# Token tiles read in quarters behind the first weights, in a one-core diffusion block

## The chip, the core and the metric

The kernel runs on one core of a Trainium2 chip. The core has five engines, each with an instruction stream of its own that is worked off in the order in which it was compiled: TensorE (PE in the profile, its weight loads PEld), VectorE (DVE), ScalarE (ACT), GpSimd (POOL) and SyncE (SP). SP computes nothing here: it issues the transfers between the chip's main memory and the core's on-chip memory. The metric is the device time of one execution in microseconds (us).

## What is computed

The reference is one layer of a diffusion transformer block in float32, with 1024 tokens of width 1024 on a grid of 16 rows by 64 columns, and 256 context tokens:

```python
sh1, sc1, g1, sh2, sc2, g2 = split(silu(c) @ w_mod + b_mod, 6)     # adaLN; likewise for c_ctx
h  = rms_norm(x, norm1) * (1 + sc1) + sh1
hc = rms_norm(ctx, norm1) * (1 + csc1) + csh1
q, k, v = split(h @ w_qkv, 3); kc, vc = (hc @ w_k), (hc @ w_v)     # q, k, kc: RMS norm per head
y = neighbourhood_attention(q, k, v, kc, vc, rpb) @ w_o            # window 8 x 16, plus the context
x = x + g1 * y
x = x + g2 * conv_ffn(rms_norm(x, norm2) * (1 + sc2) + sh2, w_up, conv, w_down)
```

## The kernel before

A float32 product is made of three products of float32r operands: each operand is split into a high part (a copy by ACT) and a low part (original minus high part, by DVE or POOL), and PE adds up high x high, high x low and low x high.

The program is written with a tile framework. Its scheduler lays out the whole program once, at compile time: it keeps its own account of when operands will be there, and puts each engine's instructions into a fixed order, by the order of the source where several are ready. On the chip an engine doesn't leave that order: if the next instruction's operand is late, everything behind it on this engine waits. A tile pool hands out a fixed number of buffers for each tag, and the next tile of a tag waits until an older one is read out.

The change lies in the first hundred microseconds of the program, in these steps:

1. **Shift and scale (lines 197 to 270).** `load_m` (L203) reads w_mod in 16 pieces `mraw` of 512 KB. For each, ACT makes the high part (`mh`, L246), DVE the low part (`ml`, L247), and PE multiplies both by the conditioning vector (L257, L258). Every fourth piece a row goes through ACT (L262) and PE (L264). The result is `s1` (L268) and `b1` (L270); no token can be modulated before b1.
2. **The first weights.** `load_w` (L211) reads w_qkv of the first pair of heads in four loads of 384 KB into the same buffers as the pieces of w_mod. `prep_w` (L138) splits them: high parts on DVE (L144), low parts on POOL (L147).
3. **Tokens.** There are ten tiles of 128 tokens, two of the context and eight of x, in the order TORD = 8, 9, 0, ..., 7. `load_x` (L165) reads one (512 KB) into one of four buffers of tag `pt`. A tile of x holds, for each of the 16 grid rows, 8 neighbouring columns, so its source is 16 runs of 32 KB, 256 KB apart. `stats_x` (L173) squares and sums it on ACT (L155; the squares themselves go to a tile that is written later anyway), takes the power -1/2 on POOL (L157) and scales the tile on DVE (L176). `transpose_x` (L178) transposes it on PE (L182), modulates it (DVE L189, ACT L191), and splits it into `hth` (ACT L193) and `htl` (DVE or POOL, L194). These twenty results lie in 20 slots of 4 KB per partition, which later parts of the kernel use again; `order` (L118) says which.
4. **First projection.** `qkv_gen(0)` (L294) makes the product of each tile with the first weights: 24 matmuls on PE (L301, L303, L305) into one of two PSUM buffers `pq`, then norms and copies (ACT L322, L329; DVE L323, L324, L330, L334, L340; POOL L325). A product's `pq` comes free when the last of these has read it. In the loop at L549 the product of tile i - AHEAD stands behind the transposes of tile i; AHEAD is 1.
5. **Loads for the attention** (L273 to L278, L365, L134, L463): the masks `mi` and `mr`, the bias table `rpb` of the first head with its sums on POOL (L371, L375), the raw weights of the second pair, and the rest of w_mod, which DVE multiplies and adds up a little at a time (`macc`, L469 and L471). The memory of these tiles comes free only when the buffers of step 2 are read out (L275 waits for L147).

Seven small constants (L223 to L235, together under 80 KB) are issued by SP between the pieces 10 and 11 of w_mod. The attention of the first head begins with the transposes at L384; from there on projections, attention, output projection and the feed-forward part follow, which the change leaves as they are.

Of the kernel before, what the change touches and what calls it, by code (L numbers as in the profile page):

```python
# [10 lines left out]
F32 = mybir.dt.float32  # L11
F32R = mybir.dt.float32r
AF = mybir.ActivationFunctionType
# [5 lines left out]
P = 128  # L19
D = 1024  # L20
KC = D // P
SEQ = 1024
CTX = 256
ROWS, COLS = 16, 64
# [6 lines left out]
NF = DFF // P  # L31
EPS = 1e-6
SCALE = DH ** -0.5
NT = NB + CTX // P
TORD = [NB, NB + 1] + list(range(NB))
BIG = 1e30
HALF = 512
MW = 256
AHEAD = 1
WB = 21  # L40
FT = -1
WS = 512
# [9 lines left out]
WD, SQD = range(8), ()  # L52
# [9 lines left out]
def block_kernel(ctx, tc, x, ctxt, cc, w_mod, b_col, b_row, n1, n2, w_qkv, gains, rpb_t, mask_i, mask_r, w_o,  # L62
                 w_up, conv_w, conv_b, w_down, comb, out):
    nc = tc.nc
    PE, ACT, DVE, POOL, SP = nc.tensor, nc.scalar, nc.vector, nc.gpsimd, nc.sync
# [11 lines left out]
    def f(ap):  # L77
        return ap.bitcast(F32)

    xv = x.rearrange("(r b j) d -> b r j d", r=ROWS, b=NB, j=8)  # L80
    ov = out.rearrange("(r b j) d -> b r j d", r=ROWS, b=NB, j=8)

    const = ctx.enter_context(pool("const"))
# [31 lines left out]
    def slot(tag, name, dt=F32R, shape=(P, D)):  # L115
        return big.tile(list(shape), dt, tag=tag, bufs=SLOTS[tag], name=name)

    order = ["gb", "t4", "t4"] + ["wa"] * 6 + ["wx"] * 2 + ["r4"] + ["rh"] * 4 + ["rl"] * 4  # L118
    hth, htl = {}, {}
    for i, t in enumerate(TORD):  # L120
        hth[t] = slot(order[2 * i], f"hth{t}", shape=(P, KC, P))
        htl[t] = slot(order[2 * i + 1], f"htl{t}", shape=(P, KC, P))
# [6 lines left out]
    ps = pstack.enter_context(pool("ps", space=PSUM))  # L129
# [20 lines left out]
    def norm_rows(t, sq, ss, sqd=False):  # L150
        if sqd:
            DVE.tensor_tensor_reduce(out=sq, in0=t, in1=t, scale=1.0, scalar=0.0, op0=ALU.mult, op1=ALU.add,
                                     accum_out=ss)
        else:
            ACT.activation(sq, t, AF.Square, accum_out=ss)  # L155
        DVE.tensor_scalar(ss, ss, 1.0 / D, EPS, ALU.mult, ALU.add)
        POOL.tensor_tensor(ss, ss, mhalf[:, 0:1], ALU.pow)  # L157

    # adaLN of the attention branch, normalised and modulated tokens, transposed and split
    att = ExitStack()  # L160
    sa = att.enter_context(pool("sa"))

    xin = {}

    def load_x(t):  # L165
        xt = sa.tile([P, D], F32, tag="pt", bufs=4, name=f"xt{t}")
        if t < NB:
            SP.dma_start(out=xt, in_=xv[t])
        else:
            SP.dma_start(out=xt, in_=ctxt[(t - NB) * P:(t - NB + 1) * P, :])  # L170
        xin[t] = xt

    def stats_x(t):  # L173
        ss = const.tile([P, 1], F32, tag="ss", bufs=3, name=f"ss{t}")
        norm_rows(xin[t], htl[t].rearrange("p a b -> p (a b)"), ss, t in SQD)
        DVE.tensor_scalar(xin[t], xin[t], ss, None, ALU.mult)  # L176

    def transpose_x(t):  # L178
# [17 lines left out]

    with pool("sm") as sm:
        segs = [1024, 1536, 0, 512]
        MB, PTM = 8, (8, 9, 10)
        AH = MB + len(PTM)  # L200
        mraw = {}

        def load_m(i):  # L203
            si, k2 = divmod(i, 4)
            if i in PTM:
                mraw[i] = sa.tile([P, 2, HALF], F32, tag="pt", bufs=4, name=f"mraw{i}")
            else:
                mraw[i] = sm.tile([P, 2, HALF], F32, tag="mraw", bufs=MB, name=f"mraw{i}")
            SP.dma_start(out=mraw[i], in_=wm[:, 2 * k2:2 * k2 + 2, segs[si]:segs[si] + HALF])

        def load_w(i):  # L211
            raw = sm.tile([P, 2, 3 * P], F32, tag="mraw", bufs=MB, name=f"wr0_{i}")
            SP.dma_start(out=raw, in_=w_qkv[0, 2 * i:2 * i + 2].rearrange("k p n -> p k n"))
            for k in range(2):
                prep_w(0, 2 * i + k, raw[:, k, :])

        for i in range(MB):
            load_m(i)
        load_x(TORD[0])
        for i in range(MB, AH):  # L220
            load_m(i)
        comb_sb = const.tile([4, 2], F32, name="comb_sb")
        SP.dma_start(out=comb_sb, in_=comb)  # L223
        bcol = const.tile([P, 48], F32, name="bcol")
        SP.dma_start(out=bcol, in_=b_col)
        n1c = const.tile([P, KC], F32, name="n1c")
        SP.dma_start(out=n1c, in_=n1)
        n2c = const.tile([P, KC], F32, name="n2c")
        SP.dma_start(out=n2c, in_=n2)
        gain_sb = const.tile([P, 2], F32, name="gain_sb")  # L230
        SP.dma_start(out=gain_sb, in_=gains)
        cw = const.tile([P, NF, 3], F32, name="cw")
        SP.dma_start(out=cw, in_=conv_w)
        cb = const.tile([P, NF], F32, name="cb")
        SP.dma_start(out=cb, in_=conv_b)  # L235
        qg = const.tile([P, 1], F32, name="qg")
        DVE.tensor_scalar(qg, gain_sb[:, 0:1], -SCALE, None, ALU.mult)
        kg = gain_sb[:, 1:2]
        pc = ps.tile([P, 2, KC, 2], F32, tag="po", bufs=1, name="pc")
        for si in range(4):  # L240
            pm = ps.tile([4, HALF], F32, tag="pq", bufs=2, name=f"pm{si}")
            for k2 in range(4):
                i = 4 * si + k2
                mh = sm.tile([P, 2, HALF], F32R, tag="mh", bufs=2, name=f"mh{i}")
                ml = sm.tile([P, 2, HALF], F32R, tag="ml", bufs=2, name=f"ml{i}")
                ACT.activation(mh, mraw[i], AF.Copy)  # L246
                DVE.tensor_tensor(ml, mraw[i], f(mh), ALU.subtract)  # L247
                if i + AH < 16:
                    load_m(i + AH)
                if 16 <= i + AH < 20:  # L250
                    load_w(i + AH - 16)
                if i in PTM:
                    load_x(TORD[1 + i - PTM[0]])
                for k in range(2):
                    kk = 2 * k2 + k
                    lw = c4[:, kk, :, :].rearrange("p a b -> p (a b)")
                    PE.matmul(pm, lw, mh[:, k, :], start=(kk == 0), stop=False)  # L257
                    PE.matmul(pm, lw, ml[:, k, :], start=False, stop=(kk == KC - 1))  # L258
                if i in (13, 14):
                    stats_x(TORD[i - 13])  # L260
            row = sm.tile([4, HALF], F32, tag="mrow", bufs=1, name=f"mrow{si}")
            ACT.activation(row, pm, AF.Copy)  # L262
            for k in range(4):
                PE.matmul(pc[:, si // 2, 4 * (si % 2) + k, :], row[:, k * P:(k + 1) * P], comb_sb, start=True,  # L264
                          stop=True)
            if si == 1:
                DVE.tensor_tensor(s1, pc[:, 0], bcol[:, 8:16].unsqueeze(2).broadcast_to([P, KC, 2]), ALU.add)
                DVE.scalar_tensor_tensor(s1, s1, 1.0, n1c.unsqueeze(2).broadcast_to([P, KC, 2]), ALU.add, ALU.mult)  # L268
            if si == 3:
                DVE.tensor_tensor(b1, pc[:, 1], bcol[:, 0:8].unsqueeze(2).broadcast_to([P, KC, 2]), ALU.add)  # L270

    # attention, with the projections of the next pair of heads in between
    sb = att.enter_context(pool("att"))  # L273
    mi = sb.tile([P, 3 * P], F32, name="mi")
    SP.dma_start(out=mi, in_=mask_i)  # L275
# [179 lines left out]
        DVE.tensor_tensor(res[a:b], po[a:b], tmp[a:b], ALU.add)  # L455
        SP.dma_start(out=o_dram[p, a:b, u * 2 * P:(u + 1) * 2 * P], in_=res[a:b])

    # adaLN of the rest, a little at a time
    def mod_gen():
        order = [2, 3, 4, 5]  # L460
        for sgi in order:
# [27 lines left out]
                        DVE.scalar_tensor_tensor(dst, dst, 1.0, n2c[:, nk * hf:nk * (hf + 1)], ALU.add, ALU.mult)  # L489
                yield  # L490

    # output projection: its first half runs beside the attention of the last heads
    xpool = ctx.enter_context(ExitStack())
    x1, wo, g1b, xsb = {}, [], [], []
    HP = NPAIR // 2
# [50 lines left out]
    mg = mod_gen()  # L546
    fill = qkv_gen(0)
    stats_x(TORD[2])
    for i, t in enumerate(TORD):  # L549
        transpose_x(t)  # L550
        if i + 4 < NT:
            load_x(TORD[i + 4])
        if i + 3 < NT:
            stats_x(TORD[i + 3])
        if i >= AHEAD:
            while (0, 1, TORD[i - AHEAD]) not in vt:
                next(fill)
# [17 lines left out]
    for si in range(ns + 4):  # L575
        if si < ns:
            p, h, t = steps[si]
# [7 lines left out]
        if si + 1 < ns and steps[si + 1][2] % 2 == 0:  # L585
            p, h, t = steps[si + 1]
# [6 lines left out]
        if 0 <= si - 3 < ns and steps[si - 3][2] % 2 == 1:  # L593
            p, h, t = steps[si - 3]
# [7 lines left out]
    filler(10 ** 6)  # L602
    att.close()

    # rest of the output projection, second norm, operands of the Winograd form (seven products of halves
    # in place of eight) of the up projection: A is w_up^T in 2 x 2 blocks, B the tokens in 2 x 2 blocks
    ff = ctx.enter_context(ExitStack())
    usb = ff.enter_context(pool("ffn"))
    BT = {}
# [1 line left out]
    for i, op in enumerate(WORD):  # L611
        for j in range(4):
            tag = btags[4 * i + j]
# [3 lines left out]
            else:  # L617
                BT[op, hl, kk] = usb.tile([P, 2, HALF], F32R, tag=tag, bufs=12 if tag == "bA" else 10,
                                          name=f"b{op}{hl}{kk}")
# [193 lines left out]
    nprep, gens, g, y, late = 2, {}, {}, {}, []  # L813
# [166 lines left out]
```

## Time and profile before

| | |
|---|---|
| median of three runs | 1492.29 us (1489.33 to 1492.66) |
| span of the profiled execution, first to last instruction | 1491.8 us |
| PE busy | 1386.5 us (93%) |
| DVE busy | 1208.1 us (81%) |
| ACT busy | 738.1 us (49%) |
| POOL busy | 805.7 us (54%) |
| moved by the DMA engines | 153.27 MB, 103 GB/s on the mean |

The profile is of one execution. Its own time is its span; the median of the runs lies 0.5 us above that. Busy times are sums over the whole span, which has stages with different limits: a stage is read from its own stretch. "A <- B" in a list of waits says that A stood idle until B was done.

### The profile page before, as it was taken

How to read it: one execution, taken by the hardware profiler on the slowest of the kernel's cores; microseconds unless marked ns; L12 is line 12 of the kernel's file. 1: busy time of each engine (PE TensorE's matmuls, PEld its weight loads, DVE VectorE, ACT ScalarE, POOL GpSimd, SP SyncE). 2: the span in 40 equal slices, each digit the busy share in tenths (PEclk: the TensorE clock that was granted, in tenths of full speed). 3: DMA queues.
4: the chain of work that ended last, by engine and by line, in shares of the span. 5: the costliest groups of instructions: out<-in, count | busy, mean ns of one | idle time of the engine just before them, and what ended most of it. 6: DMA issues, size and time to landing. Idle time of an engine off the chain costs nothing.

```text
span 1491.8 us, 22077 instructions
## 1 busy us (share of the span) xinstructions
PE 1386.5 (93%) x7396; PEld 1200.0 (80%) x7396; DVE 1208.1 (81%) x2392; ACT 738.1 (49%) x1601; POOL 805.7 (54%) x672
## 2 busy tenths in 40 slices
PE   6689999999999999999996999999999987898998
PEld 2589889898989899888885777888888865686887
DVE  6778878888888878866589889788877779988884
ACT  6575645555565656645465434344343334244541
POOL 1455544545454546744368545555545568474872
PEclk9899999999999999999997999999999998899999
DMA  9612221313131202262132132233332347433343
GB/s 315 161 37 60 64 87 55 92 51 103 49 101 45 77 14 73 69 152 76 50 129 99 64 108 101 96 106 106 107 106 99 106 137 286 155 100 127 110 131 105
DMA packets 84827, 153.27 MB, mean 103 GB/s; under 512 B 9945, under 2 KB 49001, under 8 KB 84713
## 3 DMA queue, kind: packets, MB, share of 16 engines
q1 hardware_dynamic: 84712, 151.86, 32.7%
q8 instruction: 58, 0.95, 0.3%
q14 instruction: 57, 0.46, 0.1%
HBM read 119.05 MB, written 32.78 MB: 102 GB/s over the span
## 4 chain that ended last, share of the span: by engine, by line
PE 60%; DVE 20%; DMA 7%; POOL 5%; issue 4%; ACT 3%; SPq 0%; DVEq 0%; POOLq 0%; ACTq 0%
PE pg L740 8%; PE pa L740 7%; PE sw L740 6%; PE pq L301 5%; PE pq L303 5%; PE pq L305 5%; DMA mr<-in_w_mod_dram 2%; DVE y L787 2%; DVE p L410 2%; POOL u L688 2%; PE s L398 2%; PE po L448 2%; PE po L449 2%; PE py L525 2%; PE py L526 2%
## 5 line engine op out<-in xcount | busy, mean ns | idle before, releaser
L688 POOL TENSOR_TENSOR u<-ur,u 128x512 fp32r<-128x512 f32 x154 | 231.9, 1519 | 176.8 <-ACT u L687 175.1
L417 POOL TENSOR_TENSOR p<-p,m 128x640 f32<-128x640 f32 (+1 forms) x128 | 157.3, 1230 | 157.0 <-DVE m L413 116.0
L301 PE MATMUL pq<-wh,hth 128*128 128x384 f32 (+1 forms) x640 | 219.7, 343 | 17.1 <-DVE kn L340 15.3
L305 PE MATMUL pq<-wh,htl 128*128 128x384 f32 (+1 forms) x640 | 215.2, 336 | 2.4 <-DVE htl L194 1.4
L303 PE MATMUL pq<-wl,hth 128*128 128x384 f32 (+1 forms) x640 | 215.0, 336 | 0.5 <-POOL wl L147 0.5
L687 ACT ACTIVATE u<-ur 128x512 fp32r<-128x512 f32 x154 | 93.9, 628 | 116.1 <-PE sw L740 45.4
L412 ACT ACTIVATE p<-p,m 128x640 f32<-128x640 f32 (+1 forms) x128 | 102.9, 804 | 84.3 <-DVE m L410 75.2
L301 PEld LDWEIGHTS pq<-wh,hth 128*128 128x128 f32 x640 | 124.8, 195 | 23.1 <-DVE kn L340 9.2
L325 POOL TENSOR_TENSOR qss<-qss,mhalf 128x4 f32<-128x4 f32 (+1 forms) x80 | 79.9, 999 | 97.0 <-DVE qss L324 82.8
L305 PEld LDWEIGHTS pq<-wh,htl 128*128 128x128 f32 x640 | 124.7, 195 | 3.2 <-DVE htl L194 3.2
L303 PEld LDWEIGHTS pq<-wl,hth 128*128 128x128 f32 x640 | 124.8, 195 | 1.6 <-issue 0.9
L787 DVE SCALAR_TENSOR_TENSOR y<-g,cw,y 128x896 f32<-128x896 f32 (+1 forms) x132 | 102.8, 842 | 19.2 <-ACT y L781 19.1
L449 PE MATMUL po<-pt,v 128*128 128x256 f32 x352 | 93.3, 293 | 2.1 <-DVE pt L437 2.1
L448 PE MATMUL po<-pt,v 128*128 128x256 f32 x352 | 93.8, 289 | 0.1
L895 ACT ACTIVATE db<-dr 128x512 fp32r<-128x512 f32 x77 | 47.4, 629 | 87.3 <-PE dx L911 55.7
L871 POOL TENSOR_TENSOR da<-da 128x512 fp32r<-128x512 f32 x44 | 74.9, 1725 | 27.4 <-ACT da L870 27.4
L896 POOL TENSOR_TENSOR db<-dr,db 128x512 fp32r<-128x512 f32 x44 | 64.9, 1494 | 45.6 <-ACT db L895 34.3
L410 DVE CUSTOM_DVE_ANT_0 p<-s,bias 128x640 f32<-128x640 f32 x96 | 78.3, 816 | 9.5 <-PE s L399 8.9
L436 ACT ACTIVATE pt<-pl 128x384 fp32r<-128x384 f32 (+1 forms) x128 | 58.0, 461 | 47.6 <-PE pl L429 46.6
L471 DVE SCALAR_TENSOR_TENSOR macc<-mr,cs,macc 128x256 f32<-128x256 f32 x112 | 65.0, 581 | 13.9 <-DMA mr<-in_w_mod_dram 13.0
L437 DVE TENSOR_TENSOR pt<-pl,pt 128x384 fp32r<-128x384 f32 (+1 forms) x128 | 65.4, 516 | 6.7 <-ACT pt L436 6.2
L449 PEld LDWEIGHTS po<-pt,v 128*128 128x128 f32 x352 | 66.6, 189 | 4.0 <-DVE pt L437 3.4
(258 smaller groups left out, 4184.3 us busy)
## 6 DMA issues: line engine op xcount, KB each, us to landing
ur<-in_w_up_dram SPq DMA_DIRECT2D x44, 512.0 KB
da<-act_dram SPq DMA_DIRECT2D x77, 256.0 KB
mr<-in_w_mod_dram SPq DMA_DIRECT2D x128, 128.0 KB
dr<-in_w_down_dram SPq DMA_DIRECT2D x22, 512.0 KB
wraw<-in_w_qkv_dram SPq DMA_DIRECT2D x56, 192.0 KB
mraw<-in_w_mod_dram SPq DMA_DIRECT2D x16, 512.0 KB
act_dram<-sa SPq DMA_DIRECT2D x11, 512.0 KB
act_dram<-y SPq DMA_DIRECT2D x11, 512.0 KB
```

The costliest lines, as they stand in the source:

```text
L301: PE.matmul(pq[:, c0:], hth[t][:, k, :], wh[:, c0:], start=(k == 0), stop=False)
L303: PE.matmul(pq[:, c0:], hth[t][:, k, :], wl[:, c0:], start=False, stop=False)
L305: PE.matmul(pq[:, c0:], htl[t][:, k, :], wh[:, c0:], start=False, stop=(k == KC - 1))
L410: DVE.tensor_tensor_reduce(out=dst, in0=src, in1=bb, scale=1.0, scalar=3e38, op0=ALU.add, op1=ALU.min, accum_out=m[:, 0:1])
L412: ACT.activation(w[:, :n], w[:, :n], AF.Exp, bias=m[:, 0:1], scale=-1.0, accum_out=m[:, 1:2])
L417: POOL.tensor_tensor(w[:, :n], w[:, :n], m[:, 2:3].broadcast_to([P, n]), ALU.mult)
L448: PE.matmul(po, v, th[:, j].rearrange("p a b -> p (a b)"), start=(m == 0), stop=False)
L449: PE.matmul(po, v, tl[:, j].rearrange("p a b -> p (a b)"), start=False, stop=(m == len(blks) - 1))
L687: ACT.activation(s[:, 0], r[op], AF.Copy)
L688: POOL.tensor_tensor(s[:, 1], r[op], f(s[:, 0]), ALU.subtract)
L740: PE.matmul(bank, a, b, start=(start and k == 0 and n == 0), stop=(k == 3 and n == 2), skip_group_check=True)
L787: DVE.scalar_tensor_tensor(o, i, w, o, ALU.mult, ALU.add)
```

## The change

The tokens' tiles get buffers of their own: each is read into the slot that later holds its `htl`. So all ten can be read at once, and the four `pt` buffers all go to w_mod (PTM has one piece more, pieces 12 to 15 and the weights follow by the same rule one step earlier). The second context tile is read behind piece 11. The tiles of x are read behind the last load of the first weights (`issue_after` fixes the order of two instructions on one engine), each by four transfers of 4 grid rows, 32 partitions, 128 KB. The constants are issued by POOL, ahead of everything else in that stage. The squares go into a PSUM tile, tag `s`, which the attention uses later, and stand on ACT behind the split of w_mod that was written last in the source; the first two are written at pieces 11 and 13. AHEAD becomes 3.

```diff
-AHEAD = 1
+AHEAD = 3
...
+    xraw = {t: slot(order[2 * i + 1], f"x{t}", F32) for i, t in enumerate(TORD)}
...
-    xin = {}
+    xin, queued, split = {}, [], []
+    sqj = ps.tile([P, D], F32, tag="s", bufs=1, name="sqj")
...
     def load_x(t):
-        xt = sa.tile([P, D], F32, tag="pt", bufs=4, name=f"xt{t}")
+        xt = xraw[t]
         if t < NB:
-            SP.dma_start(out=xt, in_=xv[t])
+            with tc.issue_after(queued[0].ins):
+                for g in range(0, ROWS, 4):
+                    SP.dma_start(out=xt[8 * g:8 * (g + 4)], in_=xv[t, g:g + 4])
...
-        norm_rows(xin[t], htl[t].rearrange("p a b -> p (a b)"), ss, t in SQD)
+        with tc.issue_after(split[0].ins):
+            norm_rows(xin[t], sqj, ss, t in SQD)
...
-        MB, PTM = 8, (8, 9, 10)
+        MB, PTM = 8, (8, 9, 10, 11)
...
-            SP.dma_start(out=raw, in_=w_qkv[0, 2 * i:2 * i + 2].rearrange("k p n -> p k n"))
+            queued[:] = [SP.dma_start(out=raw, in_=w_qkv[0, 2 * i:2 * i + 2].rearrange("k p n -> p k n"))]
...
+        comb_sb = const.tile([4, 2], F32, name="comb_sb")
+        POOL.dma_start(out=comb_sb, in_=comb)
...
         for i in range(MB, AH):
             load_m(i)
-        comb_sb = const.tile([4, 2], F32, name="comb_sb")
-        SP.dma_start(out=comb_sb, in_=comb)
...
+        load_x(TORD[1])
...
-                ACT.activation(mh, mraw[i], AF.Copy)
+                split[:] = [ACT.activation(mh, mraw[i], AF.Copy)]
...
-                if i in PTM:
-                    load_x(TORD[1 + i - PTM[0]])
+                if 8 <= i < 16:
+                    load_x(TORD[i - 6])
...
-                if i in (13, 14):
-                    stats_x(TORD[i - 13])
+                if i in (11, 13):
+                    stats_x(TORD[(i - 11) // 2])
...
         transpose_x(t)
-        if i + 4 < NT:
-            load_x(TORD[i + 4])
```

All seven constants move from SP to POOL in the same way as `comb_sb`.

More of the change, by code (lines that the diff above doesn't have):

```diff
@@ L212, in load_w @@
             raw = sm.tile([P, 2, 3 * P], F32, tag="mraw", bufs=MB, name=f"wr0_{i}")
-            SP.dma_start(out=raw, in_=w_qkv[0, 2 * i:2 * i + 2].rearrange("k p n -> p k n"))
+            queued[:] = [SP.dma_start(out=raw, in_=w_qkv[0, 2 * i:2 * i + 2].rearrange("k p n -> p k n"))]
             for k in range(2):
                 prep_w(0, 2 * i + k, raw[:, k, :])
+        comb_sb = const.tile([4, 2], F32, name="comb_sb")
+        POOL.dma_start(out=comb_sb, in_=comb)
+        bcol = const.tile([P, 48], F32, name="bcol")
+        POOL.dma_start(out=bcol, in_=b_col)
+        n1c = const.tile([P, KC], F32, name="n1c")
+        POOL.dma_start(out=n1c, in_=n1)
+        n2c = const.tile([P, KC], F32, name="n2c")
+        POOL.dma_start(out=n2c, in_=n2)
+        gain_sb = const.tile([P, 2], F32, name="gain_sb")
+        POOL.dma_start(out=gain_sb, in_=gains)
+        cw = const.tile([P, NF, 3], F32, name="cw")
+        POOL.dma_start(out=cw, in_=conv_w)
+        cb = const.tile([P, NF], F32, name="cb")
+        POOL.dma_start(out=cb, in_=conv_b)
         for i in range(MB):
@@ L221, in block_kernel @@
             load_m(i)
-        comb_sb = const.tile([4, 2], F32, name="comb_sb")
[L223 to L235, printed above, removed]
+        load_x(TORD[1])
         qg = const.tile([P, 1], F32, name="qg")
```

## The prediction

> **What bounds the kernel now.** I read the slices of the span first, to see where PE, which is busy for 93% of it, is not.
>
> ```profile
> PE   6689999999999999999996999999999987898998
> DVE  6778878888888878866589889788877779988884
> DMA  9612221313131202262132132233332347433343
> ```
>
> A slice is 37.3 us. PE is under 90% for several slices in a row at two places, the first three slices and the end, and in the first two the DMA engines are at their fullest. The change touches only this beginning. I take three marks from the timeline: b1 ready (L270), the first product (L301) and the attention's first transposes (L384).
>
> ```profile
> 37.38 0.16 DVE L270 TENSOR_TENSOR b<-pc,bcol 128x16 f32<-128x16 f32 x1
> ...
> 43.03 0.56 PE L301 MATMUL pq<-wh,hth 128*128 128x256 f32 x1
> ...
> 104.42 0.60 PE L384 MATMUL qt<-ident,q 128*128 128x128 f32 x4
> ```
>
> ```profile
> core 0: us, PE busy (x) PEld busy (x) DVE busy (x) ACT busy (x) POOL busy (x), PEclk, DMA share, GB/s
> 5.00:10.00 5.00, 3.00 (x7) 0.75 (x8) 2.72 (x3) 3.17 (x3) 0.00 (x0) 1.00 1.05 392
> 20.00:25.00 5.00, 4.65 (x31) 3.26 (x31) 3.52 (x5) 2.84 (x4) 0.00 (x0) 1.00 0.70 230
> 35.00:40.00 5.00, 1.05 (x8) 0.96 (x8) 4.31 (x11) 3.56 (x8) 4.94 (x6) 0.80 1.02 233
> 37.40:61.30 23.90, 11.18 (x72) 10.22 (x73) 18.91 (x48) 16.45 (x40) 13.36 (x17) 0.80 0.86 193
> 61.30:85.00 23.70, 18.87 (x106) 18.20 (x107) 17.10 (x50) 13.53 (x36) 8.72 (x11) 0.92 0.30 78
> 85.00:104.60 19.60, 19.24 (x121) 18.83 (x120) 14.88 (x47) 11.70 (x33) 10.37 (x14) 1.00 0.01 2
> 37.40:104.60 67.20, 49.29 (x297) 47.26 (x298) 50.88 (x141) 41.68 (x106) 32.46 (x41) 0.90 0.41 97
> 104.60:150.00 45.40, 43.89 (x299) 42.20 (x298) 37.20 (x108) 27.92 (x74) 24.31 (x26) 1.00 0.23 68
> ```
>
> These are two samples of the loading, one of x in flight (35 to 40), and then the stage from b1 to the attention in three stretches, as a whole, and what follows it. The stage lasts 67.2 us, in which PE does 49.29 us of work and DVE 50.88. From 85 us on PE is full (19.24 of 19.60), before that it is not, and what it lacks is told by the waits and by the chain of work that ended last.
>
> ```profile
> PE pq L301 <- DVE kn L340: 10.7, 3, 7.2
> ...
> SPq L168 <- DVE xt L176: 10.5, 1, 10.5
> ...
> DVE macc L471 <- DMA mr<-in_w_mod_dram: 2.9, 4, 1.4
> ```
>
> ```profile
> 1.19 4.01 DMA mraw<-in_w_mod_dram
> ...
> 29.68 13.35 DMA wr<-in_w_qkv_dram
> ...
> 50.24 8.13 DMA mr<-in_w_mod_dram
> ...
> 61.31 0.66 PE pq L301
> ...
> 69.50 5.08 DMA xt<-in_x_dram
> ```
>
> Three loads stand in the chain. The last first weights are issued at 29.68 behind x tiles and land at 43.0. A piece of w_mod for the running sums takes 8.13 us among x tiles; DVE stands in order before the sum that needs it, and behind it are the operations that free `pq`, so PE waits 7.2 us at one go, until 61.31. An x tile, read late because its `pt` buffer wasn't free (SP stood 10.5 us at L168 for one), takes 5.08 us alone.
>
> **The change, part by part.**
>
> *Constants on POOL.* The queue of SP shows what they cost now:
>
> ```profile
> 10.73 0.34 SPq L223 DMA_DIRECT2D comb_sb<-in_comb_dram  x1
> ...
> 18.79 0.33 SPq L235 DMA_DIRECT2D cb<-in_conv_b_dram  x1
> 20.32 2.60 SPq L209 DMA_DIRECT2D mraw<-in_w_mod_dram  x5
> 23.02 1.47 SPq L213 DMA_DIRECT2D wr<-in_w_qkv_dram  x3
> ```
>
> From 10.73 to 19.12 SP issues nothing large; at 20 to 25 us the engines carry 230 GB/s where 392 were possible, so 0.81 MB or 2.1 us are lost. That goes. The second context tile, now ahead of pieces 12 to 15, takes 512 KB / 392 GB/s = 1.3 us of it back, so b1 comes 0.8 us earlier, at 36.6. POOL never issues a load in this trace. Between the 0.33 us that SP takes and 2.5 us each, seven fit into the 17.61 us in which POOL now idles:
>
> ```profile
> 18.95 0.56 POOL L157 TENSOR_TENSOR ss<-ss,mhalf 128x1 f32<-128x1 f32 x1 [17.61 <-DVE ss L156]
> ```
>
> I take nothing. Without that cover, DVE could stand at `qg` (L237) for the gains, and 0 to 2 us of the splits with it.
>
> *First weights ahead of x.* The first piece lands at 5.2 (chain). Behind it come 15 pieces, two context tiles and four weight loads: 17 x 512 + 4 x 384 = 10,240 KB, 26.7 us at 392 GB/s, so the weights are in at 31.9 instead of 43.0. What is late next are their low parts: eight on POOL,
>
> ```profile
> L147 POOL TENSOR_TENSOR wl<-wr,wh 128x384 fp32r<-128x384 f32 x8 | 9.6, 1213 | 13.9 <-DVE wh L144 13.9
> ```
>
> 9.7 us from the first weights at about 29, so 39. The first products start some 3 to 4 us before the 43.03 of now.
>
> *x in 32 transfers into slots.* No wait for a `pt` buffer is left. SP issues 24 times more,
>
> ```profile
> 48.54 0.55 SPq L168 DMA_DIRECT2D xt<-in_x_dram  x1
> ```
>
> 8 to 13 us at 0.33 to 0.55 an issue, on a queue that stands idle for most of this stage. What a quarter costs on the DMA engines isn't in the trace. The ends, for a whole tile: 1.3 us at 392 GB/s, and the 5.08 us of the lone tile in the chain, should quarters not overlap as whole tiles do. Whole tiles of x in flight filled the engines at 233 GB/s (35 to 40 us), 2.25 us a tile. I take about 5, the slow end: a quarter fills 32 of 128 partitions, and no row shows loads of such a part keeping all the engines busy. The last tile then lands at 31.9 + 8 x 5.08 = 72.5, with 2.25 at 50.
>
> The Trainium skill (DMA: Bandwidth & Descriptors, "Why a DMA increments its semaphore by 16 and not by 1") has a rule that speaks against the quarters: a transfer from this queue runs on the largest number of engines up to 16 that divides the slowest dimension of both sides, and on the lowest-numbered ones. Four grid rows would be four engines of sixteen, where the whole tile had all; by my estimate that is a quarter of 392 GB/s, 5.35 us a tile, the last at 74.7. No run here shows it.
>
> For the sum 5 or 2.25 are the same. A tile is used up in 19.60 us / (94 / 24) = 5.0 us at the best pace of the trace, 94 matmuls of L301 to L305 being 3.9 products,
>
> ```profile
> 85.00:104.60 19.60, 17.20 (x94) 15.67 (x92) 4.28 (x19) 2.29 (x10) 1.00 0.01 2
> ```
>
> and the last square of now is made only here, so x is there in time:
>
> ```profile
> 79.01 1.05 ACT L155 ACTIVATE htl<-xt 128x1024 fp32r<-128x1024 f32 x1
> ```
>
> What the speed of x decides is the loads that SP now issues behind all of it (masks, `rpb`, second weights, w_mod for the sums): see the first rival.
>
> *Squares.* One stands ahead of two splits of w_mod:
>
> ```profile
> 17.38 1.04 ACT L155 ACTIVATE htl<-xt 128x1024 fp32r<-128x1024 f32 x1
> ...
> 18.42 2.09 ACT L246 ACTIVATE mh<-mraw 128x1024 fp32r<-128x1024 f32 x2
> ```
>
> It goes behind, worth 0 to 1.0 us; the loads set the pace of the splits, so I take 0. Whether ACT writes PSUM as fast isn't in this trace; the square has room beside DVE either way (ACT 41.68 of 67.2 us).
>
> *AHEAD 3.* Adds no work. PE has transposes of three more tiles before a product has to wait for DVE, and three products (about 13 us of PE) are left over as filling for the first attention steps.
>
> *The sum.* DVE's 50.88 us hold eight running sums (L469 once, and L471)
>
> ```profile
> L471 DVE SCALAR_TENSOR_TENSOR macc<-mr,cs,macc 128x256 f32<-128x256 f32 x7 | 3.4, 483 | 3.0 <-DMA mr<-in_w_mod_dram 2.9
> ```
>
> about 3.8 us that sit in gaps and will now come later. That leaves 47.1. DVE was 79% busy in the first stretch and 76% in the last. With the loads in time I take 81%: 58 us for the stage instead of 67.2. So 9.2 + 0.8 earlier; the 3.8 us of sums come back where PE is 97% busy and DVE 82% (104.6 to 150), half of it on the path, 1.9. Together 8.1 us. The span is 1491.8 and the runs' median 0.5 above, so **1484.2 us**. Bounds: PE alone (49.29 at 98%, plus 4 us of filling) gives 54 and at most 14 us gain, 1478; DVE at 76% gives 62, so 5.2 + 0.8 with all 3.8 back, 2.2 us, 1490.
>
> **Rivals.**
>
> *The loads behind x.* All 32 transfers have free slots, so SP will take them ahead of `mi`, whose memory opens only after the first weights are split. POOL's bias sums stand in POOL's compiled order near where the table was expected; now they start 3.0 us behind its issue:
>
> ```profile
> 47.12 0.38 SPq L366 DMA_DIRECT2D rpb<-in_rpb_t_dram  x1
> ...
> 50.12 1.69 POOL L371 TENSOR_TENSOR bias<-mr,rpb 128x128 f32<-128x128 f32 x2 [1.46 <-DMA rpb<-in_rpb_t_dram]
> 51.78 1.01 POOL L375 TENSOR_TENSOR bias<-mi,rpb 128x384 f32<-128x384 f32 x1
> 52.76 1.22 POOL L371 TENSOR_TENSOR bias<-mr,rpb 128x128 f32<-128x128 f32 x2
> ```
>
> Behind them on POOL are the powers of L325, without which no `pq` comes free. With c us a tile the table lands at 31.9 + 8c + 3.0, its sums take 3.9, and eight x products of 17.20 / 94 x 24 = 4.4 us follow: 73.9 + 8c. That passes 104.6 from c = 3.8 on. At 5.08 it is 114.5, 10 us late, 1502; the left-over products may fill gaps in the attention, 1496 then. For it: exactly this happens on DVE now (the 7.2 us). Against: the compiled order may expect slow quarters and put the table's sums late, or c may be 2.25. I give c over 3.8 a chance of 0.75 and the early place 0.45: 0.33. By the skill's rule (same page) it would be 73.9 + 8 x 5.35 = 116.7, 12 us late, 1504.
>
> *DVE sets the stage anyway.* DVE was 72 to 79% busy in every stretch, loads or not. If gaps between dependent operations, not loads, hold it there, the stage stays near 62 and the sums are given back in full: gain 0 to 3 us, 1489 to 1493. For it: 76% while no load was awaited. Against: there PE was the full one. Chance 0.14.
>
> **How the numbers follow.** About 0.2% (3.0 us) can be told from no change. Forecast 0.53, loads behind x 0.33, DVE 0.14. The forecast's own range is 1478 to 1490. For 8 in 10, I leave out its fastest end and the upper part of the first rival: 1479 to 1503. Faster by over 0.2% (under 1489.3) is the forecast, 0.53; within it the second rival and the weak end of the first, 0.15; slower 0.32.
>
> **What would show it.** Right: the last `wr` lands by 33 and the last x by about 73, products start at 38 to 40, no PE wait above 3 us up to the attention, which starts near 96. Wrong by the first rival: a wait of over 10 us for `rpb` before L371 on POOL, with products standing behind it. Wrong by the second: no load wait and L384 still after 101.

## The result, and the profile after

The changed kernel takes 1516.10 us in the median of four runs (1513.03 to 1518.98), the kernel before beside it 1490.81. The ratio is 1.0164 with a 95% interval of 1.0142 to 1.0186: 1.6% slower, where 1484.2 was forecast and the range ended at 1503. The profiled execution spans 1517.2 us against 1491.8.

The slices of the span, 37.9 us each, show the place. These are PE, the clock that it was granted and the DMA engines of the changed kernel:

```profile
PE   6369989899999999998996899999999987898998
PEclk9579999999999999999998899999999999899999
DMA  8311222213222201243132233322323237433343
```

The clock of the kernel before, for comparison:

```profile
PEclk9899999999999999999997999999999998899999
```

In the second and third slices PE is at 3 and 6 tenths, where it was at 6 and 8; in the second the clock is at half speed, where it was at 8 tenths, and the DMA engines are at 3 tenths where they stood at 6. So PE waits, and the DMA engines aren't full. The stretches of before, asked of the changed kernel:

```profile
core 0: us, PE busy (x) PEld busy (x) DVE busy (x) ACT busy (x) POOL busy (x), PEclk, DMA share, GB/s
37.40:61.30 23.90, 10.88 (x64) 10.04 (x64) 11.75 (x26) 11.00 (x24) 7.95 (x12) 0.64 0.26 102
61.30:85.00 23.70, 5.01 (x18) 4.24 (x19) 9.76 (x28) 10.83 (x26) 6.23 (x9) 0.50 0.44 143
85.00:104.60 19.60, 15.11 (x80) 14.56 (x79) 16.86 (x44) 10.84 (x28) 10.66 (x8) 0.85 0.14 42
37.40:104.60 67.20, 31.00 (x160) 28.84 (x161) 38.37 (x96) 32.67 (x78) 24.84 (x28) 0.65 0.29 99
```

While x is read (37 to 61 us), the DMA engines are busy to 0.26 and move 102 GB/s; with whole tiles in flight these were 0.86 to 1.02 and 193 to 233. A tile of 512 KB at 102 GB/s takes 5.1 us. In the next stretch PE works 5 of 23.7 us, where it worked 18.87. SP's queue and the waits of the first 130 us name what was behind it:

```profile
25.28 39.94 SPq L173 DMA_DIRECT2D x<-in_x_dram  x32
65.86 1.62 SPq L137 DMA_DIRECT2D wraw<-in_w_qkv_dram  x2
68.77 0.33 SPq L282 DMA_DIRECT2D mi<-in_mask_i_dram  x1
70.35 0.33 SPq L284 DMA_DIRECT2D mr<-in_mask_r_dram  x1
71.72 0.33 SPq L373 DMA_DIRECT2D rpb<-in_rpb_t_dram  x1
72.93 2.22 SPq L474 DMA_DIRECT2D mr<-in_w_mod_dram  x2
```

```profile
ACT sqj L156 <- DMA x<-in_x_dram: 23.8, 8, 4.0
...
PE pq L308 <- DVE kn L347: 16.4, 2, 13.8
POOL bias L378 <- DMA rpb<-in_rpb_t_dram: 16.1, 1, 16.1
...
DVE macc L476 <- DMA mr<-in_w_mod_dram: 11.3, 1, 11.3
```

Three engines stand at loads: ACT at eight squares, one for each tile of x; POOL at the bias table, which SP issued at 71.72 instead of 47.12; DVE at a piece of w_mod. How these become PE's wait of 13.8 us is read from the timeline of four engines, put in order of time (the start of each in us, how long it took, what it is, and in brackets the idle time before it and who ended it):

```profile
60.72 0.26 ACT L329 ACTIVATE qsq<-pq 128x128 f32<-128x128 f32 x1
...
63.99 0.17 DVE L331 TENSOR_SCALAR qss<-qss 128x2 f32<-128x2 f32 x1
...
76.21 1.03 ACT L156 ACTIVATE sqj<-x 128x1024 f32<-128x1024 f32 x1 [3.51 <-DMA x<-in_x_dram]
...
77.26 0.26 ACT L329 ACTIVATE qsq<-pq 128x128 f32<-128x128 f32 x1
...
78.32 0.86 POOL L378 TENSOR_TENSOR bias<-mr,rpb 128x128 f32<-128x128 f32 x2 [16.11 <-DMA rpb<-in_rpb_t_dram]
...
78.57 0.35 DVE L476 TENSOR_SCALAR macc<-mr,cs 128x256 f32<-128x256 f32 x1 [11.28 <-DMA mr<-in_w_mod_dram]
...
81.91 0.69 POOL L332 TENSOR_TENSOR qss<-qss,mhalf 128x2 f32<-128x2 f32 x1
...
82.64 0.29 DVE L347 TENSOR_TENSOR kn<-pq,qss 128x128 f32<-128x128 f32 x1 [0.95 <-POOL qss L332]
...
83.08 0.66 PE L308 MATMUL pq<-wh,hth 128*128 128x384 f32 x1 [13.83 <-DVE kn L347]
```

The first product ended at 51.5, the second at 55.6. The norm of the first was ready for POOL at 64.2, and POOL took it up at 81.91, behind the bias sums and their table. The first step on the second product (its squares, 77.26) stood on ACT behind all eight squares of x, 22 us after the product was done. Neither `pq` was free, so the third product began at 83.08.

From there on the loss stays. Counted from the trace, the attention's first transposes come 13.6 us later than before (118.00 for 104.42), the first matmul of the up projection 19.7 us (815.4 for 795.7), the end 25.4. That the distance grows after the attention's start has other reasons than the slow tiles: with the same order and fast tiles (e2 below) it grows as much.

### The profile page after: what moved, and what is told of

The parts are those of the page before. It is cut to its first block, busy times and chain, and to the rows that moved or that the text cites. A ratio compares the mean times of both kernels' runs of the same rounds, so it can differ in the third digit from the quotient of the medians.

```text
span 1517.2 us, 22163 instructions
## 1 busy us (share of the span) xinstructions
PE 1390.7 (92%) x7396; PEld 1204.2 (79%) x7396; DVE 1207.7 (80%) x2392; ACT 737.7 (49%) x1601; POOL 806.8 (53%) x679
## 5 line engine op out<-in xcount | busy, mean ns | idle before, releaser
L332 POOL TENSOR_TENSOR qss<-qss,mhalf 128x4 f32<-128x4 f32 (+1 forms) x80 | 79.0, 988 | 95.3 <-DVE qss L331 76.5
L417 DVE CUSTOM_DVE_ANT_0 p<-s,bias 128x640 f32<-128x640 f32 x96 | 78.3, 816 | 14.2 <-PE s L406 13.5
L478 DVE SCALAR_TENSOR_TENSOR macc<-mr,cs,macc 128x256 f32<-128x256 f32 x112 | 67.2, 600 | 12.0 <-DMA mr<-in_w_mod_dram 11.3
```

Source lines behind the costliest of these rows:

```text
L332: POOL.tensor_tensor(ss[:, 4 - n:], ss[:, 4 - n:], mhalf[:, 4 - n:], ALU.pow)
```

## The experiments

The theory after the result: a transfer of four grid rows runs on a quarter of the DMA engines, and the tiles at 5.1 us each, with all that stands behind them in the engines' orders, make the loss. Rivals: the number of transfers; the order as such (loads behind x, squares tied behind splits); the tiles' date rather than what stands behind it.

Each edit makes the scheduler compile a new order, and times can move by some us with it. So the pairs that tell most are those whose compiled order is the same on every engine: the changed kernel and e2_cols, g5 and h1. All numbers beside the ratios come from the traces (us):

| kernel | ratio to before, 95% interval | attention starts | up projection starts | span |
|---|---|---|---|---|
| before | | 104.4 | 795.7 | 1491.8 |
| changed | 1.0164 (1.0142 to 1.0186) | 118.0 | 815.4 | 1517.2 |
| e1_whole | 0.9972 (0.9954 to 0.9989) | 89.4 | 784.0 | 1483.7 |
| e2_cols | 1.0019 (1.0007 to 1.0031) | 94.8 | 791.9 | 1493.6 |
| e3_halves | 1.0007 (0.9990 to 1.0023) | 95.2 | 793.1 | 1492.5 |
| e4_before_quarters | 1.0154 (1.0121 to 1.0188) | 118.8 | 806.4 | 1511.8 |
| f1_ahead1 | 0.9966 (0.9952 to 0.9980) | 98.4 | 786.7 | 1484.6 |
| f2_wd | 1.0023 (1.0011 to 1.0036) | 93.7 | 791.5 | 1490.7 |
| f3_early_loads | 1.0135 (1.0117 to 1.0153) | 112.8 | 809.5 | 1509.0 |
| f4_untied | 0.9998 (0.9984 to 1.0012) | 93.7 | 788.6 | 1486.6 |
| f5_consts | 1.0006 (0.9992 to 1.0020) | 91.4 | 791.2 | 1485.5 |
| g1_wd_early | 1.0005 (0.9991 to 1.0020) | 88.2 | 788.2 | 1487.9 |
| g2_quarters_late_squares | 1.0143 (1.0123 to 1.0163) | 122.0 | 812.3 | 1514.1 |
| g4_whole_early | 1.0040 (1.0025 to 1.0055) | 96.1 | 795.3 | 1494.6 |
| g5_quarters_all | 1.0077 (1.0050 to 1.0104) | 106.0 | 803.9 | 1502.5 |
| g6_quarters_sums | 1.0110 (1.0087 to 1.0132) | 107.9 | 809.5 | 1510.1 |
| g7_whole_sums | 0.9962 (0.9942 to 0.9982) | 87.0 | 783.5 | 1480.7 |
| g8_wd_early_sums | 0.9977 (0.9960 to 0.9993) | 85.7 | 784.8 | 1484.8 |
| h1_cols_all | 1.0001 (0.9989 to 1.0014) | 97.6 | 790.4 | 1489.4 |

### The shape of the transfers

e1_whole:

```diff
-                for g in range(0, ROWS, 4):
-                    SP.dma_start(out=xt[8 * g:8 * (g + 4)], in_=xv[t, g:g + 4])
+                SP.dma_start(out=xt, in_=xv[t])
```

> The changed kernel with each token tile read by one transfer instead of four; all else (slots, place behind the first weights, constants from GpSimd, squares behind splits, AHEAD 3) stays. Engines theory (a transfer of four grid rows uses a quarter of the DMA engines, and that slow loading is what costs the 25 us): a tile takes 1.4 to 2.3 us, the last x lands by 52, rpb by 56 and the attention starts near 96 to 100, time 1484 to 1493. Order theory (whatever the tiles cost, the loads behind x and the squares tied behind splits cost it): over 1505.

e2_cols, in the same place:

```diff
+                for g in range(4):
+                    SP.dma_start(out=xt[:, 256 * g:256 * (g + 1)], in_=xv[t, :, :, 256 * g:256 * (g + 1)])
```

> The changed kernel, four transfers a tile as there, but each of 256 columns of all 128 partitions instead of all columns of 32 partitions; the compiled order of every engine is that of the changed kernel, only the shape of the 32 transfers differs. Engines theory: each transfer now has all 16 engines, the tile takes 1.4 to 2.5 us, and the time falls to that of the whole tiles, within 4 us. Theory of the number of transfers (32 issues in a row, each waiting for an earlier one): still about 5 us a tile, 1512 to 1519.

e3_halves takes `range(0, ROWS, 8)` and eight rows a transfer:

> The changed kernel with two transfers a tile, of eight grid rows (64 partitions) each. Engines theory: eight engines, 2.5 to 2.7 us a tile, last x near 54; no more than 6 us over the whole tiles. Theory of the number of transfers: half way between the whole tiles and the quarters.

The same stretch, 37.4 to 48 us, in which x is read, in the changed kernel, e1, e2 and e3:

```profile
37.40:48.00 10.60, 3.25 (x12) 2.62 (x13) 8.62 (x19) 6.23 (x14) 6.69 (x9) 0.50 0.25 102
```

```profile
37.40:48.00 10.60, 5.13 (x22) 4.51 (x23) 9.53 (x21) 7.13 (x17) 7.38 (x9) 0.52 1.04 243
```

```profile
37.40:48.00 10.60, 4.94 (x20) 4.31 (x21) 9.54 (x21) 7.69 (x19) 7.58 (x10) 0.52 0.69 205
```

```profile
37.40:48.00 10.60, 4.44 (x22) 3.73 (x22) 10.22 (x20) 6.88 (x15) 8.22 (x10) 0.60 0.51 200
```

The last two columns are the DMA share and GB/s: 0.25 and 102 for four rows, 0.51 and 200 for eight, 1.04 and 243 for all sixteen. The share is the number of grid rows over 16. That is 5.1, 2.6 and 2.2 us a tile. Four transfers by columns reach 205 GB/s at 0.69: it isn't the number of transfers. The share alone could also mean sixteen engines that are each busy a quarter of the time. The updates of the transfers' semaphores, which the traces hold, speak against it: a whole tile and a quarter by columns have sixteen each; four rows have one soon after the issue and then four, eight rows one and then eight. That fits four and eight engines which each report their own part.

The times came as the engines theory said: e1 takes 1486.62 us (its attention starts earlier than the 96 to 100 that were expected), e3 5.6 us more. e2 missed its bound, since it is 6.6 us above e1 and not within 4.

The attention's start in the changed kernel, then in e2:

```profile
118.00 0.60 PE L391 MATMUL qt<-ident,q 128*128 128x128 f32 x4
```

```profile
94.80 0.60 PE L391 MATMUL qt<-ident,q 128*128 128x128 f32 x4
```

Since e2 differs from the changed kernel in the shape of these 32 transfers and nothing else, the engines' share costs 23.6 us of span, 22.9 between the medians, 21.6 by the ratios. It is all there at the attention's start (118.0 against 94.8, 23.2) and stays to the end. This is nearly the whole of the loss. The wait of POOL for the table falls from 16.1 to 3.7 us, that of ACT for x from 23.8 to 1.2, that of DVE for w_mod from 11.3 to 0.7. e1 is 0.28% faster than before, e2 isn't: between these two lie the pace of the tiles and two compiled orders, which they don't tell apart.

e4_before_quarters puts the loop of four transfers into the kernel before:

> The kernel before with nothing changed but the four transfers a token tile. Engines theory: the tiles take 5.1 us each here too, pieces of w_mod and the first weights behind them wait for the four engines, and products start later: 1498 to 1520. If only the new place of x and its order cost the 25 us, the quarters are harmless here: 1489 to 1494.

It loses 1.5% all by itself. ACT waits for x as in the changed kernel:

```profile
ACT htl L155 <- DMA xt<-in_x_dram: 23.4, 8, 4.8
```

So the quarters cost about as much (22.8 us between the medians) in the old place of x as in the new one. What stands behind them isn't the same: here DVE also waits 5.7 us for the last of the first weights.

### What stands behind the slow tiles

These four keep the quarters at 5.1 us. f3_early_loads issues the masks, the first table and the first two pieces for the sums from POOL:

```diff
-    SP.dma_start(out=mi, in_=mask_i)
+    POOL.dma_start(out=mi, in_=mask_i)
...
-        SP.dma_start(out=rt, in_=rpb_t[hd])
+        (SP if hd else POOL).dma_start(out=rt, in_=rpb_t[hd])
...
-                    SP.dma_start(out=raw, in_=wm[:, k, s0:s0 + MW])
+                    (POOL if (sgi, hf) == (2, 0) and k < 2 else SP).dma_start(out=raw, in_=wm[:, k, s0:s0 + MW])
```

> The changed kernel with its quarters, but the two masks, the first bias table and the first two pieces of w_mod for the running sums are issued by GpSimd, so that they are not queued behind the 32 quarters on SyncE; the compiled order of the engines is nearly that of the changed kernel. Theory that the loads behind x carry the loss (POOL stood 16.1 us for rpb, DVE 11.3 us for mr): these waits go, the attention starts near 100 to 104 and the time is 1496 to 1504. Rival, that the squares on ACT, one per 5.1 us with all of ACT's later work behind them, carry it: the attention starts after 110 still, 1510 to 1518.

The attention starts at 112.8, so the rival's numbers came true: 5.2 us back and no more. The next queue was as late as the one removed:

```profile
ACT sqj L156 <- DMA x<-in_x_dram: 21.3, 8, 4.9
...
PE pt L188 <- DVE hv L195: 15.6, 3, 9.4
```

g2_quarters_late_squares adds AHEAD 1 and ties each square behind the squares `qsq` of a finished product:

```diff
+            if p == 0:
+                split[:] = [lastq]
```

> The changed kernel with its quarters at about 5.1 us a tile, the five early loads on GpSimd's queue as in f3, AHEAD 1, and each square of a token tile tied behind the sum of squares of the fifth product before it, so that ACT doesn't stand at a tile that isn't there with work behind it. Theory that the slow tiles hurt through the engines' order (squares at the head of ACT's queue, loads behind x), not through their own date: the attention starts at 98 to 104 as with whole tiles and AHEAD 1 (98.4), the time is 1486 to 1498. Rival, that 5.1 us a tile is itself too slow: the attention starts after 108, over 1503.

Against f3 the time didn't move, and the list of waits says why: ACT's wait is halved, and DVE now stands at the third piece of w_mod, which is behind x on SP still.

```profile
DVE macc L480 <- DMA mr<-in_w_mod_dram: 15.0, 1, 15.0
...
PE pt L188 <- DVE ss L157: 12.3, 1, 12.3
ACT sqj L156 <- DMA x<-in_x_dram: 11.8, 5, 4.6
```

Four products had kept pace until 71.8; the fifth began at 92.4. So the rival's numbers came true, but not by its reason: the edit took away less than it was meant to. g5_quarters_all closes that gap by tying the first running sum behind the attention's first query split (`lastql`), g6_quarters_sums does it without the tied squares and with AHEAD 3:

```diff
                     if k == 0:
-                        DVE.tensor_scalar(acc, raw, cs[:, k, 0:1], None, ALU.mult)
+                        with tc.issue_after(lastql[0].ins):
+                            DVE.tensor_scalar(acc, raw, cs[:, k, 0:1], None, ALU.mult)
```

> The kernel of g2 (quarters at 5.1 us a tile, early loads on GpSimd, AHEAD 1, squares tied behind products) with the running sums of w_mod on DVE tied behind the attention's first query split, so that no DVE operation waits for a load behind x ahead of the products. Theory that the slow tiles cost through what the engines hold behind loads: no wait over 5 us is left, the last tile's product follows the last x (about 77) by three products, the attention starts at 98 to 106, the time is 1488 to 1499. Rival, that the date of the tiles itself is the cost: the attention after 110, over 1505.

> The kernel of f3 (quarters, early loads on GpSimd, AHEAD 3, squares as in the change) with the running sums tied behind the attention's first query split. What is left of the three queues is ACT with its squares. If the squares carry most of the cost, the attention still starts after 105 and the time is 1505 to 1512; if the loads behind x carried it, 1490 to 1499.

g5's attention starts at 106.0, at the end of what the first theory allowed; its time, 1505.01 us, is past it, at the rival's bound. In its list no wait of over 1.5 us for `rpb` or `mr` is left, and that of ACT for x is 12.5 us in all, 4.5 at most. g6 starts at 107.9 and takes 1508.89, as forecast for the case that the squares carry most of it. What remained open was how much of g5's time is slow tiles and how much its remedies. h1_cols_all is g5 with the loop of e2:

> The kernel of g5 (early loads on GpSimd, AHEAD 1, squares and sums tied) with the four transfers a tile cut by columns, over all 16 engines; the compiled order of every engine is that of g5. Theory that the queues of the engines carried most of the slow tiles' cost: g5 without it is only 3 to 10 us faster, 1495 to 1502, the rest of what g5 lost being the remedies' own cost. Rival, that the tiles' date carries it whatever the engines hold: 14 us or more faster, under 1491.

It falls between the two theories, at the edge of the rival (1491.47 us where that said under 1491): 13.5 us between the medians, 11.3 by the ratios, 8.4 at the attention's start. Without the remedies the same edit was worth 23.2 at the attention's start and 21.6 by the ratios. So the remedies take away about two thirds of the slow tiles' cost at the attention's start, but less than half of it at the end: 11.3 of 21.6 us are left by the ratios, 13.1 of 23.6 by the spans. What the engines held behind late loads is one part of the loss, the date of the tiles at least as large a part of what reaches the end. The shares are not exact. AHEAD 1 is one of the remedies, and it moves the attention's start by itself (9.0 us in f1); and in g5 ACT still waits for x, with other work behind it. That the difference then grows from 8.4 to 13.1 at the end, with the same order, isn't explained; in the other pair it stayed at 23.2 to 23.6.

### The parts of the change, with whole tiles

f1_ahead1 sets AHEAD back to 1 in e1:

> The whole-tile kernel (the changed one, one transfer a token tile) with AHEAD back to 1, so that two more token tiles are multiplied by the first weights before the attention begins. Theory that AHEAD only moves two products (about 4.4 us of PE each) from before the attention to beside it: the attention starts 7 to 10 us later than 89.4 and the end is within 2 us. Rival, that the room in which PE works ahead is itself the gain: the end comes 4 us or more later.

The attention starts 9.0 us later, the end 0.9, as the first theory said. AHEAD 3 moves two products to beside the attention, and is worth nothing by itself.

f2_wd gives half of the casts to ACT (`WD = (0, 2, 4, 6)`):

> The whole-tile kernel with half of the eight casts of the first weights on ACT instead of DVE, which stood ahead of b1 on DVE (33.97 to 40.75 there) while ACT waited 3.98 us for b1. Theory that these casts hold b1 and with it the first products: b1 near 37.5 instead of 40.7, first product near 41 instead of 44.0, end 1 to 3 us earlier. Rival, that later stages take it back or the compiled order differs elsewhere: no change beyond 1.5 us, or slower.

DVE before b1 in e1, then in f2:

```profile
32.56 0.35 DVE L145 CAST wh<-wr 128x384 fp32r<-128x384 f32 x1
32.83 1.22 DVE L253 TENSOR_TENSOR ml<-mraw,mh 128x1024 fp32r<-128x1024 f32 x1
33.97 6.78 DVE L145 CAST wh<-wr 128x384 fp32r<-128x384 f32 x7
40.67 0.16 DVE L276 TENSOR_TENSOR b<-pc,bcol 128x16 f32<-128x16 f32 x1
```

```profile
33.95 3.30 DVE L145 CAST wh<-wr 128x384 fp32r<-128x384 f32 x3
37.16 0.16 DVE L276 TENSOR_TENSOR b<-pc,bcol 128x16 f32<-128x16 f32 x1
```

The date of b1 and the first product (40.7 for 44.0) came as expected, yet the attention starts 4.3 us later, and the time is the rival's. The next load was not there: POOL stood 5.6 us at `rpb` and DVE 2.75 at a piece of w_mod, behind x on SP, as in the changed kernel but smaller. g1_wd_early moves the loads as f3 does, g4_whole_early does that alone:

> The whole-tile kernel with half of the casts of the first weights on ACT (as in f2) and with the masks, the first bias table and two pieces of w_mod issued by GpSimd instead of behind x on SyncE. In f2 the products began 3.3 us earlier and then stood: DVE 2.75 us for a piece of w_mod, POOL 5.6 us for rpb. Theory that these loads ate the earlier start: both waits go, the attention starts before 90 and the end is 1480 to 1487. Rival, that the compiled order of the later stages decides: 1490 or more again.

> The whole-tile kernel with the five early loads on GpSimd's queue. With whole tiles these loads cost little there (DVE 0.67 us for a piece, POOL 0.87 us for rpb): within 2 us of the whole-tile kernel if loads alone matter; a difference of over 4 us would show how much the compiled order of later stages alone moves the time.

With both edits the attention starts at 88.2, and the time, 1491.44 us, is that of before: the early start was lost again further on, and the rival was right. g4 has no wait for a load of over 1.5 us in this stage, and is 0.7% slower than e1. Its compiled order is another one, in which PE stood 6.25 us at 73 to 79 us for operations of DVE. f4_untied takes the squares' tie out of e1:

> The whole-tile kernel without the tie of the squares behind the splits of w_mod. Theory that the tie is worth nothing in itself: within 2 us of the whole-tile kernel. Rival, that it is what keeps the splits and b1 early: b1 and the first product 1 to 3 us later and the time 2 to 4 us longer.

0.3% slower than e1 by the ratios, 5.2 us between the medians, with b1 at 41.0 for 40.7: both theories missed. The splits don't suffer, as the first said, but the time is longer; the rest of the stage is in another order, and whether that is the reason isn't shown. f5_consts puts the constants back on SP, with hardly a row changed elsewhere:

> The whole-tile kernel with the seven constants back on SyncE; the compiled order of the other engines is the same but for a few rows. Forecast's theory: on SyncE they cost 2.1 us of loading, so the last piece of w_mod, b1 and the products come 1 to 2 us later, the end 0.5 to 2 us later. Rival, that the constants on GpSimd slow the pieces of w_mod by as much as SyncE loses: no difference in the date of b1 and none beyond 1 us in the time.

b1 comes at 41.8, 1.1 us later, the attention 2.0, the span 1.8; the ratio differs by 0.34%, 5 us, with intervals that do not meet. So the constants on POOL are a gain; its size lies between the 1.8 us of the spans and those 5, which is more than was forecast.

g7_whole_sums and g8_wd_early_sums tie the sums in e1 and in g1 as g5 does:

> The whole-tile kernel with the running sums tied behind the attention's first query split. With fast tiles they waited 0.67 us for a load, so that tying them should bring 0 to 3 us at the start of the attention and take it back later: 1483 to 1491.

> The kernel of g1 (whole tiles, half of the casts on ACT, early loads on GpSimd) with the running sums tied likewise; the try at a version better than the whole-tile kernel: attention at 85 to 88, 1480 to 1488 if the start decides; 1490 or more if the later stages' compiled order does.

Both times are as expected, 1486.35 and 1487.24 us. g7 has the lowest ratio of all, 0.9962, but its interval covers the ratio of e1. A version that beats both kernels, the one before by 0.3%, is thus the change with x read by whole tiles.

## Why the prediction was wrong, by its steps

- **x in 32 transfers.** This is the step that failed, and not in the pace: about 5 us a tile was taken and 5.1 came. That the two are so close is luck: the 5.08 was the time from issue to landing of one whole tile, with pieces of w_mod beside it, and the 5.1 is the pace of quarters on fewer engines. It failed at "For the sum 5 or 2.25 are the same" and "x is there in time". With the compiled order unchanged, 5.1 us a tile and the fast tiles of e2 (205 GB/s, 2.6 us a tile) differ by 22 to 24 us. The argument used the last square of before, at 79.01, and the last one did come earlier, at 76.21. But ACT works in a fixed order, and in the new one all squares stood ahead of work on products that were long done. Not the date of the last tile alone counted, but every tile's date against what stood behind it. And with most of what stood behind them taken away (g5, h1) slow tiles still cost 11 to 14 us, so their date counts for itself too.
- **The loads behind x.** This rival had a chance of 0.33, and its mechanism is what POOL shows: 16.1 us for `rpb`, with the powers of L332 behind it; 5.1 us a tile was past the 3.8 from which it was to bite. It forecast 1496 to 1504. What its price lacked were the two other queues with the same fault at the same time (ACT's squares, DVE's sums); taking away one or two (f3, g2) brought 3 to 5 us, as long as one was left. The table's date was nearly right (75.5 by its formula, its sums began at 78.32), and so was the attention's (114.5 at 5.08 us a tile, 118.00 measured), but the latter by luck: the formula has eight products of 4.4 us behind the table, 35.1 us, and in the trace it was five that took 34.9 (83.1 to 118.0), since AHEAD 3 leaves three for later and the five stood and waited. What its 1502 us lacked is for the most part what is lost behind the attention's start.
- **The Trainium skill's rule** (DMA: Bandwidth & Descriptors, "Why a DMA increments its semaphore by 16 and not by 1"), as many engines as divide the slowest dimension of both sides: the traces agree for 4, 8 and 16 rows, with 0.25, 0.51 and 1.04 of the engines' time. The prediction's estimate by it was 5.35 us a tile; 5.1 was measured.
- **Constants on POOL.** Right in its sign. POOL spent 0.53 to 0.72 us on an issue, in idle time, but the last piece of w_mod landed at 29.33 for 29.61, 0.3 us sooner instead of 0.8: the fourth and fifth pieces came 0.7 and 1.2 us later beside the constants, and at 5 to 10 us the engines moved 341 GB/s where it had been 392.
- **First weights ahead of x.** They landed at 33.8 for 31.9, against 43.0 before. The products started at 45.86, not at 38 to 40: b1 was at 40.85 instead of 36.6, since seven casts of the first weights stood ahead of it on DVE, 6.77 us in all. No step had asked what DVE holds ahead of b1 once the weights are early. f2 shows it, and shows too that this start is worth nothing by itself.
- **Squares.** "Worth 0 to 1.0 us" holds for fast tiles at most; with slow ones they are ACT's 23.8 us of waits.
- **AHEAD.** Right that it adds no work; it moves two products past the attention's start.
- **The sum.** With whole tiles the span is 1483.7, 8.1 us under before, which is the number of the sum, but by luck and not by its terms: b1 came 3.3 us later instead of 0.8 earlier, and the stage from b1 to the attention took 48.7 us instead of 58, of which f1 gives 9.0 to AHEAD. By the ratio the gain is 4.2 us. A second step failed here: that an earlier start of the attention reaches the end but for 1.9 us. e2 starts it at 94.8, close to the 96 of the prediction, and still ends 1.8 us later than before. The sum puts the products that AHEAD moves behind that start at nothing; by f1 and e1, which differ in AHEAD alone, 9.0 us at the attention's start are 0.9 at the end.
- **Growth after the attention.** Not foreseen. e2, with fast transfers, starts the attention 9.6 us earlier than before, the up projection 3.8 us earlier, and ends 1.8 us later. The changed kernel has the same order and loses the same distance. AHEAD's two products can account for the first part (in f1 and e1 the 9.0 us between the attention's starts are 2.7 at the up projection). What the 5.6 us behind the start of the up projection come from isn't shown: the compiled order is another one there too, and no experiment takes that apart.

## What to carry to other kernels

Cut a transfer so that 16 are left in the slowest dimension of its source, as the columns do here, and read the DMA share: transfers that queue up while the engines are busy to only 0.25 were on four engines here. Before a load is moved ahead of others, go through each engine's compiled order for the first instruction that waits for a load behind it; if several engines hold one, removing one shows little (3 to 5 us of some 25 here). Compare kernels whose compiled order is the same where a few us matter, since another order went with up to 0.7% here, where no load was waited for (g4).

## What the runs showed of the hardware

A wait of PE cost more than its length here. After the 13.83 us the changed kernel's product ran like this:

```profile
83.53 0.52 PE L310 MATMUL pq<-wl,hth 128*128 128x384 f32 x1
...
88.02 0.52 PE L308 MATMUL pq<-wh,hth 128*128 128x384 f32 x1
88.33 0.46 PE L310 MATMUL pq<-wl,hth 128*128 128x384 f32 x1
88.63 0.34 PE L312 MATMUL pq<-wh,htl 128*128 128x384 f32 x1
88.81 0.34 PE L308 MATMUL pq<-wh,hth 128*128 128x384 f32 x1
```

For 5.4 us the matmuls start 0.32 us apart, then 0.17. The granted clock of the stretch was 0.50. After a wait of 2.62 us the product at 101.73 has its matmuls 0.32 us apart from 102.40 on, and the next one 0.17 from 105.75 on. The Trainium skill (TensorE: Matmul & The Clock Gate, "Part 1: The HAM clock gate") has half the clock after at least one idle window of some 3.4 us, and the full one after at least one busy window of the same length; the half agrees, from the product's start to the full pace it took 5.4 us in the one case and 4.0 in the other.

The eight casts of the first weights on DVE in e1 (shortest, median and longest in ns, then the first and the last start):

```profile
L145 DVE CAST wh<-wr x8: 347/1144/1171, 32.6 to 39.6; 128x384 fp32r<-128x384 f32 x8
```

Two of them, at 32.56 and 35.06, began while POOL did nothing, and took 0.35 us. The other six ran while POOL made the low parts of the same weights, and took 1.14 to 1.17.

Whole tiles of x, 16 runs of 32 KB that lie 256 KB apart, came at 243 GB/s with the engines busy all the time (1.04), where pieces of w_mod came at 392 GB/s (5 to 10 us of the kernel before).
